# LayerNorm of a 2048x2048x2048 matmul: the opening rows' last chunk of A is transposed by the DMA and used last, and row tile 5 is loaded and transposed ahead of gamma and beta

## The chip, the cores and the metric

The kernel runs on one core of one Trainium2 chip. Five engines work side by side, each in its own order: TensorE (PE, with its weight loads as PEld), VectorE (DVE), ScalarE (ACT), GpSimd (POOL) and SyncE (SP), which here issues most of the transfers; 16 DMA engines move the data. The metric is the time of one execution in device microseconds (us), as a median over runs.

## The reference

```python
m, k, n = 2048, 2048, 2048          # a: (m, k), b: (k, n), float32
x = np.matmul(a, b)
mean = np.mean(x, axis=-1, keepdims=True)
var = np.var(x, axis=-1, keepdims=True)
normalized = (x - mean) / np.sqrt(var + eps)
return (gamma * normalized + beta).astype(np.float32)
```

## The kernel before, in words

The 2048 rows of the output are 16 row tiles of 128. N is cut into 4 quarters of 512 columns, K into 16 steps `kt` of 128, and four steps make a chunk. One matmul (`mm`, L85) adds one `kt` of one row tile and one quarter, 128x512, into a bank of PSUM, of which there are eight. A and B arrive in float32 and are multiplied in float16. B stays in SBUF as `b16`. A must stand with K on the partitions, so its tiles are transposed into `at`, two row tiles to a buffer.

While B is still arriving, the first five row tiles (R = 5, the opening rows) are worked on together, so that each piece of B that lands feeds five matmuls. Their A comes in chunks of 512 columns: `load_a1` and `load_a2` load to the staging buffers (`stg`, six of 512 KB) and VectorE casts to `a16s` (L186, L194). Then `turn` transposes on TensorE against an identity (L243) and ScalarE copies the result from PSUM to `at` (L245). B comes through `load_b2`, two `kt` of one quarter at a time, 512 KB, cast by VectorE (L205). SP issues the loads strictly in the order of the code; each waits until the staging buffer that it is to fill has been cast.

The order in the opening: chunk 0 of quarters 0, 1 and 2 for the five rows, each put aside into `x` in SBUF by ScalarE (`put_aside`, L261). Then the whole of quarter 3 (`MAIN`), with the transposes of chunks 1, 2 and 3 placed between its matmuls by `spots`; it is copied out by `evacuate` (ScalarE L95, and VectorE's statistics L96). Then chunks 1 to 3 of quarters 0 and 1, step by step over the five rows first and row by row at the end (`k_row`), with the remaining pieces of B asked for at hand-set places by `bring`. A finished quarter is added to the part put aside and its statistics taken (`add_rest`, VectorE L265 and L266). Quarter 2 is done row by row in the last loop of the opening, which also closes each row: `stats` (L102, L104 on VectorE, a square root L106 on ScalarE) and `queue_norm`, which queues the row's normalization in halves on a backlog.

The other eleven row tiles follow one by one, four quarters of 16 matmuls each. After each quarter `evacuate` runs and `drain(1)` issues one half of a queued row: two passes of VectorE (`centre` L111, `scale` L117) and a store. Their A is loaded by GpSimd's queue with a cast to float16 on the way (L345, three buffers `a16`), and transposed by one DMA for a whole row, 128x2048 (`turn_ahead`, L428, issued by SP two tiles ahead). A copy of one column on GpSimd (`gate`, L255) lets these loads start only when the last piece of B has landed. gamma and beta are broadcast to 128 partitions by two loads on SP (L335, L336) behind the last load of B. The last row tile has an ending of its own (`finish_row`).

The order of every engine is the order of the code (a manual schedule). What the change touches: `load_b2` L201 to L206, the loading loop L222 to L230, `bring` L248 to L255, the loops of `MAIN` and of the quarters L308 to L333, the loading of rows L342 to L345, `turn_ahead` L424 to L431 and the closing loop L432 to L436.

Of the kernel before, what the change touches and what calls it, by code (L numbers as in the profile page):

```python
# [10 lines left out]
FP16 = mybir.dt.float16  # L11
AluOp = mybir.AluOpType
# [4 lines left out]
def kernel(  # L17
# [21 lines left out]
    n_kc = n_kt // KC  # L39
    R = 5  # L40
    ASIDE, MAIN = (0, 1, 2), 3
# [10 lines left out]
    a16p = ctx.enter_context(tc.tile_pool(name="a16p", bufs=3))  # L52
# [22 lines left out]

    def new_pair(g):
        pair[g] = atp.tile([P, 2, n_kt, P], FP16, tag="at", name=f"at{g}")

    def at(i):
        return pair[i // 2][:, i % 2]  # L80

    def mm(i, q, kt, first, last):
        if (i, q) not in acc:
            acc[i, q] = bank(f"acc{i}_{q}")
        nc.tensor.matmul(  # L85
            acc[i, q], at(i)[:, kt, :], b16[:, kt, ds(q * NB, NB)],
            start=first, stop=last,
        )

    def evacuate(i, q):  # L90
        if xs[i] is None:
            xs[i] = xpool.tile([P, N], FP32, tag="x", name=f"x{i}")
            bnst[i] = stat.tile([P, n_nb, 6], FP32, tag="bnst", name=f"bnst{i}")
        qs = ds(q * NB, NB)
        nc.scalar.copy(xs[i][:, qs], acc[i, q])  # L95
        nc.vector.bn_stats(bnst[i][:, q, :], xs[i][:, qs])  # L96
# [3 lines left out]
    def stats(i):  # L100
        mv = stat.tile([P, 2], FP32, tag="mv", name=f"mv{i}")
        nc.vector.bn_aggr(mv, bnst[i])  # L102
        ve = stat.tile([P, 1], FP32, tag="ve", name=f"ve{i}")
        nc.vector.tensor_tensor(ve, mv[:, 1:2], eps_t, AluOp.add)  # L104
        sq = stat.tile([P, 1], FP32, tag="sq", name=f"sq{i}")
        nc.scalar.activation(sq, ve, ActFn.Sqrt)  # L106
        return mv, sq

    def centre(i, q, mv):
        qs = ds(q * NB, NB)  # L110
        nc.vector.scalar_tensor_tensor(  # L111
            xs[i][:, qs], xs[i][:, qs], mv[:, 0:1], gamma_b[:, qs],
            AluOp.subtract, AluOp.mult)

    def scale(i, q, rstd):
        qs = ds(q * NB, NB)
        nc.vector.scalar_tensor_tensor(  # L117
            xs[i][:, qs], xs[i][:, qs], rstd, beta_b[:, qs],
            AluOp.mult, AluOp.add)

    def store(i, q0, nq):
        s = ds(q0 * NB, nq * NB)
        nc.sync.dma_start(out[ts(i, P), s], xs[i][:, s])

    def inv(i, sq):
        rstd = stat.tile([P, 1], FP32, tag="rstd", name=f"rstd{i}")
        nc.vector.reciprocal(rstd, sq)
        return rstd

    def queue_norm(i, mv, sq):  # L130

        got = {}

        def piece(q0):
            def run():
                centre(i, q0, mv)
                centre(i, q0 + 1, mv)
                if q0 == 0:
                    got["rstd"] = inv(i, sq)
                scale(i, q0, got["rstd"])  # L140
                scale(i, q0 + 1, got["rstd"])
                store(i, q0, 2)
            return run

        backlog.extend(piece(q) for q in range(0, n_nb, 2))
# [20 lines left out]
    a16_of = {}  # L166
# [15 lines left out]
    def load_a1(i, c):  # L182
        st = half_stage()
        nc.sync.dma_start(st, a[ts(i, P), ts(c, KW)])  # L184
        a16_room(i, c)
        nc.vector.tensor_copy(a16_of[i, c], st)  # L186

    def load_a2(i, c):
        st = stg.tile([P, 2, NB], FP32, tag="st", name=f"sta{i}_{c}")
        nc.sync.dma_start(  # L190
            st, a[ds(i * P, 2 * P), ts(c, KW)].rearrange("(t p) k -> p t k", p=P))
        for m in (0, 1):
            a16_room(i + m, c)
        nc.vector.tensor_copy(held["a"][:, ds(i % KC, 2), :], st)  # L194
# [3 lines left out]
        nc.sync.dma_start(st, b[ts(k, P), 0:NB])  # L198
        nc.vector.tensor_copy(b16[:, k, 0:NB], st)  # L199

    def load_b2(k, q):  # L201
        st = stg.tile([P, 2, NB], FP32, tag="st", name=f"stb{q}_{k}")
        nc.sync.dma_start(
            st, b[ds(k * P, 2 * P), ds(q * NB, NB)].rearrange("(t p) n -> p t n", p=P))
        nc.vector.tensor_copy(b16[:, k:k + 2, ds(q * NB, NB)], st)  # L205
        return st  # L206

    pairs = [list(range(i, min(i + 2, R))) for i in range(0, R, 2)]

    def load_pair(j, c):  # L210
        if len(pairs[j]) == 2:
            load_a2(pairs[j][0], c)
        else:
            load_a1(pairs[j][0], c)
# [3 lines left out]
    for q in ASIDE[1:]:  # L218
        load_b2(0, q)
        load_b2(2, q)  # L220
    load_pair(0, 1)
    for c in range(n_kc):  # L222
        load_b2(c * KC, MAIN)
        if c + 1 < n_kc:
            load_pair(0 if c > 0 else 1, c + 1)
        load_b2(c * KC + 2, MAIN)
        if c + 1 < n_kc:
            if c > 0:
                load_pair(1, c + 1)
            load_pair(2, c + 1)  # L230

    warm = bank("warm")

# [4 lines left out]
    def turn(rows, c):  # L238
        n = len(rows)
        t_ps = psum.tile([P, n, KC, P], FP16, tag="ps", name=f"tps{rows[0]}_{c}")  # L240
        for m, i in enumerate(rows):
            for j in range(KC):
                nc.tensor.transpose(t_ps[:, m, j, :], a16_of[i, c][:, ts(j, P)], ident)  # L243
        i0 = rows[0]
        nc.scalar.copy(  # L245
            pair[i0 // 2][:, ds(i0 % 2, n), ds(c * KC, KC), :], t_ps)

    later = [(k, q) for q in ASIDE for k in range(0 if q == MAIN else KC, n_kt, 2)]  # L248

    def bring(n):  # L250
        for _ in range(n):
            k, q = later.pop(0)
            st = load_b2(k, q)
            if not later:
                nc.gpsimd.tensor_copy(gate, st[:, 0, 0:1])  # L255

    def put_aside(p, q):
        if xs[p] is None:
            xs[p] = xpool.tile([P, N], FP32, tag="x", name=f"x{p}")
            bnst[p] = stat.tile([P, n_nb, 6], FP32, tag="bnst", name=f"bnst{p}")  # L260
        nc.scalar.copy(xs[p][:, ds(q * NB, NB)], acc.pop((p, q)))  # L261

    def add_rest(p, q):
        qs = ds(q * NB, NB)
        nc.vector.tensor_tensor(xs[p][:, qs], acc[p, q], xs[p][:, qs], AluOp.add)  # L265
        nc.vector.bn_stats(bnst[p][:, q, :], xs[p][:, qs])  # L266
# [23 lines left out]
    for q in ASIDE[1:]:  # L290
# [3 lines left out]
        for p in range(R):  # L294
            for kt in range(2, KC):
                mm(p, q, kt, False, kt == KC - 1)
            put_aside(p, q)


    spots = {(0, 4): 0, (1, 1): 1, (1, 4): 2}  # L300
    for h in (0, 1):
# [3 lines left out]
            if (h, p) in spots:  # L305
                turn(pairs[spots[h, p]], 1)
    spots = {(1, 4): 0, (2, 4): 1, (3, 1): 2}
    for kt in range(KC, n_kt - KC):  # L308
        for p in range(R):
            mm(p, MAIN, kt, False, False)  # L310
            if (kt % KC, p) in spots:
                turn(pairs[spots[kt % KC, p]], kt // KC + 1)
    for kt in range(n_kt - KC, n_kt - 2):
        for p in range(R):
            mm(p, MAIN, kt, False, False)
    for p, n in enumerate((1, 1, 0, 1, 0)):
        for kt in (n_kt - 2, n_kt - 1):
            mm(p, MAIN, kt, False, kt == n_kt - 1)
        bring(n)
        evacuate(p, MAIN)  # L320


    for q, k_row, ahead, asked in (
            (0, n_kt - KC, 7, (0, 0, 1, 0, 1)), (1, 2 * KC, 2, (0, 1, 1, 1, 1))):
        bring(ahead)
        for kt in range(KC, k_row):
            for p in range(R):
                mm(p, q, kt, kt == KC, False)
        for p in range(R):
            for kt in range(k_row, n_kt):  # L330
                mm(p, q, kt, False, kt == n_kt - 1)
            bring(asked[p])
            add_rest(p, q)  # L333
    assert not later
    nc.sync.dma_start(gamma_b, gamma.unsqueeze(0).to_broadcast([P, N]))  # L335
    nc.sync.dma_start(beta_b, beta.unsqueeze(0).to_broadcast([P, N]))  # L336
    if eps_ap is not None:
# [1 line left out]
    else:  # L339
        nc.vector.memset(eps_t, eps_val)  # L340

    a16 = {}  # L342
    for i in range(R, n_mt):
        a16[i] = a16p.tile([P, K], FP16, tag="a16", name=f"a16_{i}")
        nc.gpsimd.dma_start(a16[i], a[ts(i, P), :])  # L345


    rows_gb = [stg.tile([2, 2, NB], FP32, tag="st", name=f"gb{h}") for h in (0, 1)]
# [72 lines left out]
        queue_norm(i, mv, sq)  # L421
        drain(1)

    def turn_ahead(t):  # L424
        if R <= t < n_mt:
            if t % 2 == 0:
                new_pair(t // 2)
            nc.sync.dma_start_transpose(at(t), a16[t])  # L428

    turn_ahead(R)  # L430
    turn_ahead(R + 1)  # L431
    for p in range(R):  # L432
        for kt in range(KC, n_kt):
            mm(p, ASIDE[2], kt, kt == KC, kt == n_kt - 1)
        add_rest(p, ASIDE[2])
        queue_norm(p, *stats(p))  # L436
    for i in range(R, n_mt):
        last = i == n_mt - 1
        turn_ahead(i + 2)
# [49 lines left out]
```

## Time and profile before

| | us |
|---|---|
| median of 3 runs (lowest to highest) | 245.42 (245.38 to 245.78) |
| the profiled execution | 245.69 |
| its span in the trace | 243.7 |
| TensorE matmuls, busy | 235.0 (96%) |
| VectorE busy | 173.0 (71%) |
| ScalarE busy | 55.1 (23%) |
| GpSimd busy | 12.6 (5%) |

In the profile a line such as L85 is the line of the kernel that issued the instruction, `out<-in` are the tiles it writes and reads. A group's row gives count, busy time and the mean duration of one in ns, then the time its engine had been idle before it and who ended that. Durations of pipelined matmuls overlap, so the mean of one (379 ns) is longer than the step from one to the next.

### The profile page before, as it was taken

What the parts mean: (1) busy time and instruction counts of PE and PEld (TensorE: products, weight loads), DVE (VectorE), ACT (ScalarE), POOL (GpSimd) and SP (SyncE); (2) the same over time, 40 slices, a digit from 0 to 9 for tenths busy, and PEclk for the clock granted to TensorE, in tenths of its full rate; (3) what the DMA queues carried; (4) which work ended last, traced back from release to release, by engine and by line L of the source; (5) the groups of instructions that cost most, each with busy time, mean ns of one, the idle gap of its engine ahead of it and who ended that gap; (6) DMA issues with size and microseconds to landing.
All of it is one profiled execution on the core that took longest, in us unless ns stands there. A gap on an engine that the chain in (4) does not pass through costs nothing.

```text
span 243.7 us, 2983 instructions
## 1 busy us (share of the span) xinstructions
PE 235.0 (96%) x1137; PEld 108.3 (44%) x1137; DVE 173.0 (71%) x304; ACT 55.1 (23%) x104; POOL 12.6 (5%) x19
## 2 busy tenths in 40 slices
PE   6899999999999999999999999999999999999991
PEld 2344555444444444444444444444444444444440
DVE  1544454969997679999999995937558392946771
ACT  2466445500000011112121211112111121112132
POOL 0000000000210100000000000036000000000000
PEclk9999999999999999999999999999999999999996
DMA  4999999999999998888999797683907145120405
GB/s 122 393 389 384 384 350 392 386 335 370 360 266 204 150 139 242 237 186 251 241 224 256 143 290 177 192 202 74 256 5 180 78 115 146 58 114 0 175 1 172
DMA packets 41190, 52.64 MB, mean 216 GB/s; under 512 B 24404, under 2 KB 24404, under 8 KB 40920
## 3 DMA queue, kind: packets, MB, share of 16 engines
q1 hardware_dynamic: 39592, 46.68, 59.1%
q0 software_dynamic: 1584, 5.77, 15.3%
q8 instruction: 9, 0.15, 0.3%
q14 instruction: 5, 0.04, 0.1%
HBM read 35.67 MB, written 16.78 MB: 215 GB/s over the span
## 4 chain that ended last, share of the span: by engine, by line
PE 93%; DMA 2%; ACT 1%; DVE 1%; SPq 0%; issue 0%
PE acc L85 91%; DMA st<-in_a_dram 2%; PE tps L243 2%; ACT x L408 1%; DVE bnst L373 0%; PE y L396 0%; DVE a16s L186 0%; PE warm L236 0%; SPq L198 0%; SPq L184 0%; PE ms_ps L391 0%; ACT mv_last L389 0%; DVE mv_last L388 0%; ACT lead L392 0%
## 5 line engine op out<-in xcount | busy, mean ns | idle before, releaser
L85 PE MATMUL acc<-b,at 128*128 128x512 f16 x1024 | 223.2, 379 | 1.0 <-DVE b L199 0.9
L85 PEld LDWEIGHTS <-at 128*128 128x128 f16 x1024 | 99.6, 98 | 119.3 <-ACT at L245 1.3
L96 DVE BATCH_NORM_STATS2 bnst<-x 128x6 f32<-128x512 f32 x48 | 32.9, 689 | 33.9 <-ACT x L95 33.8
L95 ACT COPY x<-acc 128x512 f32<-128x512 f32 x48 | 27.7, 588 | 108.8 <-PE acc L85 107.5
L117 DVE SCALAR_TENSOR_TENSOR x<-x,rstd,beta_b 128x512 f32<-128x512 f32 x62 | 43.8, 747 | 0.6
L111 DVE SCALAR_TENSOR_TENSOR x<-x,mv,gamma_b 128x512 f32<-128x512 f32 x60 | 42.0, 741 | 0.0
L205 DVE CAST b<-stb 128x1024 f16<-128x1024 f32 x30 | 20.4, 688 | 11.0 <-DMA stb<-in_b_dram 10.9
L106 ACT ACTIVATE sq<-ve 128x1 f32<-128x1 f32 x15 | 3.0, 203 | 51.1 <-DVE ve L104 51.1
L245 ACT COPY at<-tps 128x512 f16<-128x512 f16 (+1 forms) x14 | 10.6, 769 | 14.3 <-PE tps L243 14.0
L265 DVE TENSOR_TENSOR x<-acc,x 128x512 f32<-128x512 f32 x15 | 10.3, 685 | 3.3 <-PE acc L85 3.3
L345 POOL DMA_DIRECT2D a<-in_a_dram x11 | 6.4, 583 | 91.1 <-DMA at<-a 90.8
L266 DVE BATCH_NORM_STATS2 bnst<-x 128x6 f32<-128x512 f32 x15 | 10.4, 695 | 0.5
L261 ACT COPY x<-acc 128x512 f32<-128x512 f32 x15 | 7.6, 607 | 5.1 <-PE acc L85 5.1
L186 DVE CAST a16s<-st 128x512 f16<-128x512 f32 x8 | 3.4, 427 | 6.4 <-DMA st<-in_a_dram 6.2
L243 PE MATMUL tps<-ident,a16s 128*128 128x128 f16 x80 | 6.8, 220 | 0.9 <-DVE a16s L186 0.8
L236 PE MATMUL warm<-zeros 128*128 128x512 f16 x19 | 6.2, 462 | 1.2 <-DVE zeros L152 1.2
L243 PEld LDWEIGHTS <-a16s 128*128 128x128 f16 x80 | 5.2, 98 | 4.7 <-DVE a16s L186 2.6
L194 DVE CAST a16s<-sta 128x1024 f16<-128x1024 f32 x6 | 4.2, 694 | 4.1 <-DMA sta<-in_a_dram 3.4
L357 POOL TENSOR_SCALAR gb<-gb 1x1024 f32<-1x1024 f32 x2 | 5.5, 2764 | 0.0
L102 DVE BATCH_NORM_AGGREGATE mv<-bnst 128x2 f32<-128x24 f32 x15 | 4.0, 264 | 0.5
L236 PEld LDWEIGHTS <-zeros 128*128 128x128 f16 x19 | 2.0, 115 | 4.2 <-issue 2.6
L255 POOL COPY gate<-stb 128x1 f32<-128x1 f32 x1 | 0.2, 183 | 63.5 <-DMA stb<-in_b_dram 63.5
(31 smaller groups left out, 22.8 us busy)
## 6 DMA issues: line engine op xcount, KB each, us to landing
stb<-in_b_dram SPq DMA_DIRECT2D x30, 512.0 KB, 6.5
out_dram<-x SPq DMA_DIRECT2D x30, 512.0 KB, 3.0
a<-in_a_dram POOLq DMA_DIRECT2D x11, 512.0 KB, 6.7
sta<-in_a_dram SPq DMA_DIRECT2D x6, 512.0 KB, 6.3
st<-in_a_dram SPq DMA_DIRECT2D x8, 256.0 KB, 7.4
st<-in_b_dram SPq DMA_DIRECT2D x4, 256.0 KB, 6.6
gamma_b<-in_gamma_dram SPq DMA_DIRECT2D x1, 1024.0 KB, 7.2
beta_b<-in_beta_dram SPq DMA_DIRECT2D x1, 1024.0 KB, 9.2
```

The costliest lines, as they stand in the source:

```text
L85: nc.tensor.matmul(acc[i, q], at(i)[:, kt, :], b16[:, kt, ds(q * NB, NB)], start=first, stop=last,)
L95: nc.scalar.copy(xs[i][:, qs], acc[i, q])
L96: nc.vector.bn_stats(bnst[i][:, q, :], xs[i][:, qs])
L111: nc.vector.scalar_tensor_tensor(xs[i][:, qs], xs[i][:, qs], mv[:, 0:1], gamma_b[:, qs], AluOp.subtract, AluOp.mult)
L117: nc.vector.scalar_tensor_tensor(xs[i][:, qs], xs[i][:, qs], rstd, beta_b[:, qs], AluOp.mult, AluOp.add)
L205: nc.vector.tensor_copy(b16[:, k:k + 2, ds(q * NB, NB)], st)
L236: nc.tensor.matmul(warm if to is None else to, zeros[:, 0:P], zeros, start=True, stop=True)
L243: nc.tensor.transpose(t_ps[:, m, j, :], a16_of[i, c][:, ts(j, P)], ident)
L245: nc.scalar.copy(pair[i0 // 2][:, ds(i0 % 2, n), ds(c * KC, KC), :], t_ps)
L261: nc.scalar.copy(xs[p][:, ds(q * NB, NB)], acc.pop((p, q)))
L265: nc.vector.tensor_tensor(xs[p][:, qs], acc[p, q], xs[p][:, qs], AluOp.add)
L266: nc.vector.bn_stats(bnst[p][:, q, :], xs[p][:, qs])
```

## The change

The A of the opening rows' chunk 3 is still loaded and cast as before, but no longer transposed by TensorE: five DMA transposes of 128x512 (`turn_last`) write it to `at`, issued by SP between loads of B. Chunk 3's loads stand later among the loads, behind the first pieces of quarter 0. Since chunk 3 comes later, the main quarter now stops after chunk 2 and is put aside, and so is quarter 0 a second time (`add_part`, which adds to what is already aside, without statistics). Quarters 1 and 2 are done to their end. Chunk 3 of quarters 3 and 0 is multiplied last, row by row, and closes the rows.

The remaining 14 loads of B are issued one after another, with no hand-set places, and ScalarE casts them instead of VectorE. Row tile 5 is loaded once B's quarter 2 has landed, with four loads of B still behind it, and transposed ahead of gamma and beta; the loads of row tiles 6 and on wait for the very last load of B.

```diff
-    def load_b2(k, q):
+    def load_b2(k, q, cast=nc.vector.tensor_copy):
...
-        nc.vector.tensor_copy(b16[:, k:k + 2, ds(q * NB, NB)], st)
+        cast(b16[:, k:k + 2, ds(q * NB, NB)], st)
...
-    for c in range(n_kc):
+    K3 = n_kt - KC
+    for c in range(n_kc - 1):
         load_b2(c * KC, MAIN)
-        if c + 1 < n_kc:
+        if c + 2 < n_kc:
             load_pair(0 if c > 0 else 1, c + 1)
         load_b2(c * KC + 2, MAIN)
-        if c + 1 < n_kc:
+        if c + 2 < n_kc:
             if c > 0:
                 load_pair(1, c + 1)
             load_pair(2, c + 1)
+    load_b2(KC, 0)
+    load_b2(KC + 2, 0)
+    for j in range(len(pairs)):
+        load_pair(j, n_kc - 1)
+        if j < 2:
+            load_b2(2 * KC + 2 * j, 0)
+    load_b2(KC, 1)
+    load_b2(KC + 2, 1)
...
+    def turn_last(i):
+        nc.sync.dma_start_transpose(at(i)[:, ds(K3, KC), :], a16_of[i, n_kc - 1])
...
+    def add_part(p, q):
+        qs = ds(q * NB, NB)
+        nc.vector.tensor_tensor(xs[p][:, qs], acc.pop((p, q)), xs[p][:, qs], AluOp.add)
...
+    def part(q, k0, k1, k_row, done):
+        for kt in range(k0, k_row):
+            for p in range(R):
+                mm(p, q, kt, kt == k0, False)
+        for p in range(R):
+            for kt in range(k_row, k1):
+                mm(p, q, kt, kt == k0, kt == k1 - 1)
+            done(p, q)
...
-    for p, n in enumerate((1, 1, 0, 1, 0)):
-        for kt in (n_kt - 2, n_kt - 1):
-            mm(p, MAIN, kt, False, kt == n_kt - 1)
-        bring(n)
-        evacuate(p, MAIN)
+    for p in range(R):
+        for kt in (K3 - 2, K3 - 1):
+            mm(p, MAIN, kt, False, kt == K3 - 1)
+        put_aside(p, MAIN)
...
+    later = [(k, 1) for k in range(2 * KC, n_kt, 2)]
+    later += [(k, 2) for k in range(KC, n_kt, 2)]
+    later += [(k, q) for q in (MAIN, 0) for k in range(K3, n_kt, 2)]
+    for n, (k, q) in enumerate(later):
+        for i in range(2 * n, min(2 * n + 2, R)):
+            turn_last(i)
+        st = load_b2(k, q, nc.scalar.copy)
+        if (k, q) in ((n_kt - 2, 2), later[-1]):
+            nc.gpsimd.tensor_copy(gate, st[:, 0, 0:1])
+        if (k, q) == (n_kt - 2, 2):
+            load_row(R)
+    turn_ahead(R)
+    part(0, KC, K3, K3 - 2, add_part)
+    part(1, KC, n_kt, K3, add_rest)
+    part(2, KC, n_kt, K3, add_rest)
     nc.sync.dma_start(gamma_b, gamma.unsqueeze(0).to_broadcast([P, N]))
     nc.sync.dma_start(beta_b, beta.unsqueeze(0).to_broadcast([P, N]))
...
-    for i in range(R, n_mt):
-        a16[i] = a16p.tile([P, K], FP16, tag="a16", name=f"a16_{i}")
-        nc.gpsimd.dma_start(a16[i], a[ts(i, P), :])
+    for i in range(R + 1, n_mt):
+        load_row(i)
...
-    turn_ahead(R)
     turn_ahead(R + 1)
-    for p in range(R):
-        for kt in range(KC, n_kt):
-            mm(p, ASIDE[2], kt, kt == KC, kt == n_kt - 1)
-        add_rest(p, ASIDE[2])
+    def close_opening(p, q):
+        add_rest(p, q)
         queue_norm(p, *stats(p))
+    part(MAIN, K3, n_kt, K3, add_rest)
+    part(0, K3, n_kt, K3, close_opening)
```

More of the change, by code (lines that the diff above doesn't have):

```diff
@@ L246, in turn @@
             pair[i0 // 2][:, ds(i0 % 2, n), ds(c * KC, KC), :], t_ps)
[L248 to L255, printed above, removed]
+    def turn_last(i):
+        nc.sync.dma_start_transpose(at(i)[:, ds(K3, KC), :], a16_of[i, n_kc - 1])
     def put_aside(p, q):
@@ L307, with load_row, turn_ahead @@
     spots = {(1, 4): 0, (2, 4): 1, (3, 1): 2}
-    for kt in range(KC, n_kt - KC):
+    for kt in range(KC, K3 - 2):
         for p in range(R):
             mm(p, MAIN, kt, False, False)
-            if (kt % KC, p) in spots:
+            if kt < 2 * KC and (kt % KC, p) in spots:
                 turn(pairs[spots[kt % KC, p]], kt // KC + 1)
-    for kt in range(n_kt - KC, n_kt - 2):
-        for p in range(R):
-            mm(p, MAIN, kt, False, False)
-    for p, n in enumerate((1, 1, 0, 1, 0)):
-        for kt in (n_kt - 2, n_kt - 1):
-            mm(p, MAIN, kt, False, kt == n_kt - 1)
-        bring(n)
-        evacuate(p, MAIN)
[L323 to L334, printed above, removed]
+    for p in range(R):
+        for kt in (K3 - 2, K3 - 1):
+            mm(p, MAIN, kt, False, kt == K3 - 1)
+        put_aside(p, MAIN)
+    a16 = {}
+    def load_row(i):
+        a16[i] = a16p.tile([P, K], FP16, tag="a16", name=f"a16_{i}")
+        nc.gpsimd.dma_start(a16[i], a[ts(i, P), :])
+    def turn_ahead(t):
+        if R <= t < n_mt:
+            if t % 2 == 0:
+                new_pair(t // 2)
+            nc.sync.dma_start_transpose(at(t), a16[t])
+    later = [(k, 1) for k in range(2 * KC, n_kt, 2)]
[13 more added lines that the diff above has]
+    part(2, KC, n_kt, K3, add_rest)
     nc.sync.dma_start(gamma_b, gamma.unsqueeze(0).to_broadcast([P, N]))
@@ L340 @@
         nc.vector.memset(eps_t, eps_val)
-    a16 = {}
-    for i in range(R, n_mt):
-        a16[i] = a16p.tile([P, K], FP16, tag="a16", name=f"a16_{i}")
-        nc.gpsimd.dma_start(a16[i], a[ts(i, P), :])
+    for i in range(R + 1, n_mt):
+        load_row(i)
     rows_gb = [stg.tile([2, 2, NB], FP32, tag="st", name=f"gb{h}") for h in (0, 1)]
@@ L422, in close @@
         drain(1)
[L424 to L428, printed above, removed]
-    turn_ahead(R)
     turn_ahead(R + 1)
-    for p in range(R):
-        for kt in range(KC, n_kt):
-            mm(p, ASIDE[2], kt, kt == KC, kt == n_kt - 1)
-        add_rest(p, ASIDE[2])
+    def close_opening(p, q):
+        add_rest(p, q)
         queue_norm(p, *stats(p))
+    part(MAIN, K3, n_kt, K3, add_rest)
+    part(0, K3, n_kt, K3, close_opening)
     for i in range(R, n_mt):
```

## The prediction, made before the changed kernel ran

> **What bounds the kernel now.** I read the chain that ended last first, then its pieces in order of time, then the waits of TensorE.
>
> ```profile
> PE 93%; DMA 2%; ACT 1%; DVE 1%; SPq 0%; issue 0%
> ...
> 10.54 14.68 PE acc L85 x67
> ...
> 36.09 0.45 PE tps L243 x8
> 36.53 1.08 PE acc L85 x5
> 37.61 0.45 PE tps L243 x8
> 38.06 0.43 PE acc L85 x2
> 38.49 0.22 PE tps L243 x4
> 38.72 195.77 PE acc L85 x907
> ```
>
> The first line is the page's summary of the chain, the others are the start, duration and work of single pieces. From 10.54 us TensorE is the chain: 907 matmuls stand in one piece of 195.77 us, 0.2158 us each, with nothing between them. The last chunk's transposes stand in the chain too: 8, 8 and 4 of them take 0.45, 0.45 and 0.22 us.
>
> ```profile
> PE warm L236 <- DVE zeros L152: 1.2, 1, 1.2
> PE acc L85 <- DVE b L199: 0.9, 1, 0.9
> PE tps L243 <- DVE a16s L186: 0.8, 1, 0.8
> PE y L396 <- ACT lead L392: 0.4, 1, 0.4
> ```
>
> These are all waits of TensorE: three in the opening's first microseconds, one in the tail. So between 10.54 and 234 us time falls only if TensorE does less, and it rises only if the change makes TensorE wait.
>
> ```profile
> 40.00:50.00 10.00, 10.00 (x49) 4.52 (x47) 7.48 (x13) 3.83 (x6) 0.00 (x0) 1.00 1.04 382
> 50.00:60.00 10.00, 10.00 (x48) 4.58 (x47) 8.55 (x14) 0.00 (x0) 0.00 (x0) 1.00 1.00 353
> 60.00:70.00 10.00, 10.00 (x48) 4.50 (x47) 9.51 (x16) 0.00 (x0) 2.36 (x4) 1.00 0.99 346
> ```
>
> Columns: the stretch, its length, busy time of PE, PEld, DVE, ACT and POOL, granted clock, DMA share, GB/s. While TensorE is full, the DMA engines are full as well (share 1.04, 382 GB/s). The opening thus runs with two full resources side by side, and the change moves work from the first to the second.
>
> **What is removed.** 20 transposes of chunk 3: 0.45 + 0.45 + 0.22 = 1.12 us of the chain. The number of matmuls stays 1024. If nothing takes the freed place, the time falls by 1.12 us.
>
> **How early the operands come.** The loads are served one after the other; VectorE's casts show when they land.
>
> ```profile
> 32.01 0.69 DVE L205 CAST b<-stb 128x1024 f16<-128x1024 f32 x1 [0.82 <-DMA stb<-in_b_dram]
> 50.08 0.69 DVE L205 CAST b<-stb 128x1024 f16<-128x1024 f32 x1 [0.63 <-DMA stb<-in_b_dram]
> ...
> L245 ACT COPY at<-tps 128x1024 f16<-128x1024 f16 x6 | 6.1, 1012 | 7.5 <-PE tps L243 7.5
> L95 ACT COPY x<-acc 128x512 f32<-128x512 f32 x48 | 27.7, 588 | 108.8 <-PE acc L85 107.5 <-DMA out_dram<-x 1.3
> ```
>
> The first cast takes B's rows 8 and 9 of the main quarter, the second comes 13 loads of 512 KB and one of 256 KB later: 18.07 / 13.5 = 1.34 us a load. The order up to the first of them is unchanged, and in the new order the load for quarter 1, kt 14 and 15, is also 13.5 loads behind it. It lands at 50.08 plus whatever the five DMA transposes ahead of it cost. Its cast is now ScalarE's, which the trace does not show in this shape: below by VectorE's 0.69, above by two 512-wide copies, 1.18; I take 1.01 from the copy of the same size. Ready: 51.09 + 5T, with T the time that one transpose of 128x512 holds up the loads.
>
> TensorE needs it when it has done, after 36.09, 10 matmuls of the main quarter, 40 of quarter 0 and 42 of quarter 1: 36.09 + 92 x 0.2158 = 55.94. So up to 4.85 us can be absorbed, T = 0.97. By the same count kt 12 is needed at 55.51 and ready at 49.75 + 5T, kt 10 at 53.35 against 48.41 + 4T, kt 8 at 51.20 against 47.07 + 2T. Kt 14 is the tightest. Quarter 2's first pair is ready at 52.43 + 5T and needed at 59.83, later ones have more. Ahead of the transposes the slack is over 1 us everywhere: the load for kt 10 of the main quarter, for instance, moves one place forward and is cast by 34.04, against 36.09.
>
> **What a transpose costs.** The trace has only full-row ones (128x2048, four times as much).
>
> ```profile
> L428 SPq DMA_TRANSPOSE at<-a x11: 1869/3254/5823, 72.5 to 198.2; - x11
> DMA to landing us min/median/max: 4.4/5.0/13.6
> ...
> 79.91 0.53 POOL L345 DMA_DIRECT2D a<-in_a_dram x1 [12.08 <-DMA at<-a]
> 82.37 0.53 POOL L345 DMA_DIRECT2D a<-in_a_dram x1 [1.93 <-DMA at<-a]
> 93.50 0.53 POOL L345 DMA_DIRECT2D a<-in_a_dram x1 [10.60 <-DMA at<-a]
> 106.83 0.53 POOL L345 DMA_DIRECT2D a<-in_a_dram x1 [12.80 <-DMA at<-a]
> ...
> 101.37 3.21 SPq L428 DMA_TRANSPOSE at<-a  x1
> ...
> 104.00:105.00 1.00, 1.00 (x6) 0.44 (x5) 1.00 (x3) 0.00 (x0) 0.00 (x0) 1.00 1.17 218
> ```
>
> GpSimd's loads wait for transposes to free a buffer, so their starts date the landings. The first two transposes end 2.46 us apart though each takes 4.4 us or more from issue to landing: latency overlaps, and what a following transfer feels is 2.46 us, or 0.62 a quarter. The window inside the transpose issued at 101.37 agrees: 218 GB/s at full share, so 0.131 MB take 0.60 us. Lower end: as fast as a load of that size, 1.34 / 4 = 0.34. Upper end: the third one's distance, 93.50 - 82.37 = 11.13, or 2.78. Three of these readings lie near 0.6, so I take T = 0.62. 5T = 3.1 us against 4.85: hidden behind the lead of the loads, with 1.75 us to spare. The Trainium skill (Advanced Engine Details and Errata, X-Bar Transpose) says that such a transpose is as fast as a regular DMA; this trace does not agree (218 against 382 GB/s). By the rule 5T would be an estimated 1.7 us, and the rival below that holds up the loads would lose its chance.
>
> SP issues one full row in 3.25 us (median), so a quarter in 0.81 and five in 4.1. Each waits for its cast. Two go out behind the quarter 1, kt 6 load, two behind kt 8, one behind kt 10. The loads queued behind them on SP are delayed by less than 4.85 even if all of it counts, and some six loads' work is already in the queues. The load for kt 14 also waits until the first transpose has landed.
>
> **The other moves.** Five statistics of the main quarter move to the end, and five more adds come there. With 40 matmuls still to do (8.63 us), VectorE has more than that:
>
> ```profile
> L266 DVE BATCH_NORM_STATS2 bnst<-x 128x6 f32<-128x512 f32 x15 | 10.4, 695 | 0.5
> L265 DVE TENSOR_TENSOR x<-acc,x 128x512 f32<-128x512 f32 x15 | 10.3, 685 | 3.3 <-PE acc L85 3.3
> L102 DVE BATCH_NORM_AGGREGATE mv<-bnst 128x2 f32<-128x24 f32 x15 | 4.0, 264 | 0.5
> ...
> 150.00:155.00 5.00, 5.00 (x25) 2.27 (x24) 2.65 (x7) 0.79 (x2) 0.00 (x0) 1.00 0.90 198
> ```
>
> Ten rows at 1.38 us and five closings make some 16 us, so VectorE is about 6 us further behind when row tile 5 starts. Row tile 5's first bank was that of the main quarter's third row. Quarter 2's first row ends at 69.3; five pairs and then two and a half of the main quarter later it is free: 79.7. TensorE asks for it at 81.4. Later banks have more room, being asked for again eight quarters (27.6 us) after they were filled. The lag is worked off in the gaps VectorE has from 150 us on. Cost 0; if the 1.7 us cover were gone, TensorE would stand there. ScalarE's 14 casts (14 us) fall into a stretch where it is idle (0.00 from 50 to 70), again cost 0.
>
> Row tile 5's load moves ahead of four of B's, its transpose ahead of gamma and beta:
>
> ```profile
> 65.10 0.18 POOL L255 COPY gate<-stb 128x1 f32<-128x1 f32 x1 [63.52 <-DMA stb<-in_b_dram]
> 65.65 2.18 POOL L345 DMA_DIRECT2D a<-in_a_dram  x3 [0.37 <-DVE x L265]
> 72.46 12.78 SPq L428 DMA_TRANSPOSE at<-a  x3
> ```
>
> The gate opens at 50.08 + 6 x 1.34 + 3.1 = 61.2; with 0.55 to the issue and 6.81 (65.65 to 72.46) the row is there at 68.6. As long as the first one (72.46 to 79.91) the transpose ends at 76.0, against 81.4. SP waits for that load with gamma, beta and the next transposes queued behind; gamma and beta go out some 13 us later than before and are wanted by VectorE only after its 16 us of adds, about 92. Cost 0.
>
> **Sum.** 245.69 us of the profiled execution (243.7 span, 1.99 around it) less 1.12 is 244.57. The median of the runs shown is 0.27 below the profiled one: 245.42 - 1.12 = 244.3.
>
> **The rivals.**
>
> *The transposes hold up the loads* (the other side). If each holds the queue as long as the one at 101.37 held its buffer, (106.83 - 101.37) / 4 = 1.37, five make 6.83, TensorE waits 1.98 us at quarter 1, kt 14, and the time is 246.3. It is slower than before from T above 1.19 (0.97 plus 1.12 / 5), and at 2.78 it gives 9.05 us of waiting, 253.4. For it: the 11.13 us of the third one, next to other transfers. Against: the 2.46 us and the 218 GB/s. Chance 0.24, of which 0.04 within 0.2% of before.
>
> *Each transpose costs its full latency.* The trace's shortest landing is that of the last row's stores:
>
> ```profile
> out_dram<-x SPq DMA_DIRECT2D x4, 256.0 KB, 2.5
> ```
>
> With T = 2.5 us TensorE waits 12.5 - 4.85 = 7.65: 252.0. Against it: landings 2.46 us apart for four times the data. Chance 0.04. The Trainium skill (DMA: Bandwidth & Descriptors, Anatomy of one DMA) gives a fixed 2.0 us for a DMA from GpSimd's path, an estimated 2.3 for this size; it also calls it a latency, and so does the trace.
>
> *Row tile 5 is late.* If its transpose takes the 13.6 us of the slowest, it lands at 82.2, TensorE waits 0.8 and the time is 245.1, no change. Chance 0.05.
>
> *VectorE gives the bank late.* At 1.85 us a row in place of 1.38 the bank is free at 82.9: 1.5 us of waiting, 245.8, again within 0.2%. Nothing in the profile makes a pair that slow. Chance 0.02.
>
> *The change gives nothing:* the freed 1.12 us turn into a wait of the same size for B elsewhere in the opening, 245.4. Slack of over 1 us at each load speaks against it. Chance 0.03.
>
> **How the numbers follow.** Forecast 0.62, rivals together 0.38. Faster by over 0.2% (about 0.5 us, what a measurement here can tell from no change): 0.62; within: 0.04 + 0.05 + 0.02 + 0.03 = 0.14; slower: 0.20 + 0.04 = 0.24. The likeliest case alone spans 244.0 to 244.7; the range has to take in the loads held up at 1.37, so 244.0 to 246.4.
>
> **What would show it.** Right: no wait of the accumulating matmuls on casts, on the opening's transposes or on adds; 60 transposes left on TensorE; casts for quarter 1, kt 14, ending near 54 us. Wrong: a wait of TensorE for a ScalarE cast between 50 and 56 us (T too small), for row tile 5 near 81, or for an add there.

## The result, and the profile after

The changed kernel takes 244.38 us (median of 8 runs, 244.04 to 245.1), the kernel before on the same chip 245.49 (8 runs, 245.2 to 245.86): a ratio of 0.9958, 95% interval 0.9947 to 0.9969, or 1.1 us less. The profiled execution took 244.29 us with a span of 242.2, where the one before had 245.69 and 243.7. Ratios here are taken over fast runs alone, which leaves out one execution (249.53 us, of `e6_gb_first`).

The chain that ended last comes first again, in order of time (start, duration, work); the first line is the page's summary.

```profile
PE 94%; DMA 2%; ACT 1%; DVE 1%; issue 0%; DVEq 0%
...
9.97 14.67 PE acc L85 x67
...
32.48 0.22 PE tps L252 x4
32.70 13.61 PE acc L85 x63
...
46.50 0.69 DVE x L268
...
47.24 8.36 PE acc L85 x38
55.60 0.04 issue
55.64 177.59 PE acc L85 x822
```

TensorE is still the chain, and the pieces of 0.45, 0.45 and 0.22 us that the last chunk's transposes had in it are gone. In their place are two interruptions. At 46.3 us quarter 1 wants a bank which VectorE's `add_part` (L268) has not yet read. At 55.6 it wants quarter 1's `kt` 14, which ScalarE is just casting. How much they cost is seen beside a second execution of the same kernel, in which both are missing:

```profile
33.23 0.22 PE tps L252 x4
33.46 200.09 PE acc L85 x927
```

From the same point, the end of the last transposes on TensorE, 927 matmuls take 200.09 us here. In the first execution they would have ended at 32.70 + 200.09 = 232.79 and ended at 55.64 + 177.59 = 233.23: 0.44 us were lost. TensorE itself is idle for no more than 0.08 and 0.04 us of this; the rest is overlap between neighbouring matmuls that is missing at a stop.

So the two profiled executions, before and after, compare as follows. TensorE's matmuls ended at 38.72 + 195.77 = 234.49 before and at 233.23 after, 1.26 us earlier: 1.12 by the transposes, 0.57 because the dense part happened to begin at 9.97 in place of 10.54, less the 0.44. (The opening up to there is the same code, and over the traces of this study it begins between 9.97 and 10.94.) Of the difference of 1.40 between the two times the remaining 0.14 lies behind the matmuls: a tail 0.24 shorter, and 0.10 more outside the span.

The groups of instructions by line (count | busy us, mean ns | idle before) show that the work on TensorE is what was announced:

```profile
L85 PE MATMUL acc<-b,at 128*128 128x512 f16 x1024 | 223.0, 379 | 0.1
...
L252 PE MATMUL tps<-ident,a16s 128*128 128x128 f16 x60 | 5.4, 225 | 0.1
...
L205 ACT CAST b<-stb 128x1024 f16<-128x1024 f32 x14 | 14.6, 1045 | 16.8 <-DMA stb<-in_b_dram 16.8
```

1024 matmuls, 60 transposes left, and ScalarE's 14 casts at 1.045 us each. Of SyncE's queue the stretch with the five transposes, then the transposes' durations in ns (min/median/max):

```profile
37.67 2.70 SPq L258 DMA_TRANSPOSE at<-a16s  x2
40.47 0.53 SPq L203 DMA_DIRECT2D stb<-in_b_dram  x1
41.09 4.46 SPq L258 DMA_TRANSPOSE at<-a16s  x2
45.60 0.58 SPq L203 DMA_DIRECT2D stb<-in_b_dram  x1
46.27 1.20 SPq L258 DMA_TRANSPOSE at<-a16s  x1
...
L258 SPq DMA_TRANSPOSE at<-a16s x5: 1201/1347/2601, 37.7 to 46.3; - x5
```

SP stands 1.2 to 2.6 us at each transpose, 0.53 to 0.58 at a load. The five take 2.70 + 4.46 + 1.20 = 8.36 us of it. What this does to the loads is dated by the casts, first VectorE's, then ScalarE's (start, duration, idle before and its releaser):

```profile
31.02 0.69 DVE L205 CAST b<-stb 128x1024 f16<-128x1024 f32 x1 [0.82 <-DMA stb<-in_b_dram]
...
45.29 0.69 DVE L205 CAST b<-stb 128x1024 f16<-128x1024 f32 x1 [2.14 <-DMA stb<-in_b_dram]
...
54.54 1.04 ACT L205 CAST b<-stb 128x1024 f16<-128x1024 f32 x1 [0.75 <-DMA stb<-in_b_dram]
```

The first is the main quarter's `kt` 8, the second quarter 1's `kt` 6, on which VectorE waits 2.14 us with the adds L268 queued behind it: the first interruption. The third is quarter 1's `kt` 14. It ends at 55.58. The last 822 matmuls take 177.59 of the 200.09 us, so undisturbed TensorE would have begun them 22.50 us behind 32.70, at 55.20: the second.

Row tile 5 is dated by GpSimd, whose fourth load waits for its transpose, and by SP's issue of that transpose:

```profile
63.39 0.19 POOL L357 COPY gate<-stb 128x1 f32<-128x1 f32 x1 [61.81 <-DMA stb<-in_b_dram]
63.95 0.72 POOL L340 DMA_DIRECT2D a<-in_a_dram  x1 [0.37 <-issue]
...
80.35 0.53 POOL L340 DMA_DIRECT2D a<-in_a_dram  x1 [9.67 <-DMA at<-a]
...
70.95 6.88 SPq L346 DMA_TRANSPOSE at<-a  x1
```

The row is there at 70.95 and transposed by 80.3. Row tile 5 begins 118 matmuls (822 less its and the later rows' 704) after 55.64, at 81.1. Only 0.8 us lie between.

### The profile page after: what moved, and what is told of

It reads as the page before. It is cut to its first block, busy times and chain, and to the rows that moved or that the text cites. A ratio compares the mean times of both kernels' runs of the same rounds, so it can differ in the third digit from the quotient of the medians.

```text
span 242.2 us, 2970 instructions
## 1 busy us (share of the span) xinstructions
PE 235.4 (97%) x1117; PEld 107.5 (44%) x1117; DVE 171.6 (71%) x300; ACT 66.0 (27%) x115; POOL 12.5 (5%) x20
## 4 chain that ended last, share of the span: by engine, by line
PE 94%; DMA 2%; ACT 1%; DVE 1%; issue 0%; DVEq 0%
PE acc L85 91%; DMA st<-in_a_dram 2%; PE tps L252 2%; PE warm L245 1%; ACT x L437 1%; DVE bnst L402 0%; DVE x L268 0%; PE y L425 0%; DVE a16s L186 0%; PE ms_ps L420 0%; ACT mv_last L418 0%; DVE mv_last L417 0%; ACT lead L421 0%; DVEq L268 0%
## 5 line engine op out<-in xcount | busy, mean ns | idle before, releaser
L85 PE MATMUL acc<-b,at 128*128 128x512 f16 x1024 | 223.0, 379 | 0.1
L85 PEld LDWEIGHTS <-at 128*128 128x128 f16 x1024 | 99.8, 98 | 120.2 <-ACT at L254 1.1
L117 DVE SCALAR_TENSOR_TENSOR x<-x,rstd,beta_b 128x512 f32<-128x512 f32 x62 | 44.4, 756 | 0.6
L111 DVE SCALAR_TENSOR_TENSOR x<-x,mv,gamma_b 128x512 f32<-128x512 f32 x60 | 42.9, 756 | 0.0
L95 ACT COPY x<-acc 128x512 f32<-128x512 f32 x43 | 24.5, 585 | 66.9 <-PE acc L85 66.9
L272 DVE TENSOR_TENSOR x<-acc,x 128x512 f32<-128x512 f32 x20 | 13.6, 678 | 13.6 <-PE acc L85 13.6
L205 DVE CAST b<-stb 128x1024 f16<-128x1024 f32 x16 | 11.1, 694 | 12.5 <-DMA stb<-in_b_dram 12.5
L205 ACT CAST b<-stb 128x1024 f16<-128x1024 f32 x14 | 14.6, 1045 | 16.8 <-DMA stb<-in_b_dram 16.8
L264 ACT COPY x<-acc 128x512 f32<-128x512 f32 x20 | 10.2, 605 | 7.5 <-PE acc L85 7.5
L254 ACT COPY at<-tps 128x512 f16<-128x512 f16 (+1 forms) x11 | 8.1, 742 | 10.8 <-PE tps L252 10.5
L245 PE MATMUL warm<-zeros 128*128 128x512 f16 x19 | 7.4, 534 | 1.2 <-DVE zeros L152 1.2
L252 PEld LDWEIGHTS <-a16s 128*128 128x128 f16 x60 | 4.0, 100 | 3.6 <-DVE a16s L186 2.2
L252 PE MATMUL tps<-ident,a16s 128*128 128x128 f16 x60 | 5.4, 225 | 0.1
```

The source lines that it names most:

```text
L85: nc.tensor.matmul(acc[i, q], at(i)[:, kt, :], b16[:, kt, ds(q * NB, NB)], start=first, stop=last,)
L111: nc.vector.scalar_tensor_tensor(xs[i][:, qs], xs[i][:, qs], mv[:, 0:1], gamma_b[:, qs], AluOp.subtract, AluOp.mult)
L117: nc.vector.scalar_tensor_tensor(xs[i][:, qs], xs[i][:, qs], rstd, beta_b[:, qs], AluOp.mult, AluOp.add)
L205: cast(b16[:, k:k + 2, ds(q * NB, NB)], st)
L245: nc.tensor.matmul(warm if to is None else to, zeros[:, 0:P], zeros, start=True, stop=True)
L254: nc.scalar.copy(pair[i0 // 2][:, ds(i0 % 2, n), ds(c * KC, KC), :], t_ps)
```

## The experiments

Each edit is made against the changed kernel. All compare with the kernel before, run on the same chip beside them.

| kernel | median us (lowest to highest, runs) | ratio to before, 95% interval |
|---|---|---|
| `e1_pe_turn` | 245.68 (245.05 to 247.05, 12) | 1.0004 [0.9986, 1.0022] |
| `e2_no_turn` | 244.21 (244.09 to 244.61, 5) | 0.9940 [0.9927, 0.9953] |
| `e3_twice` | 250.87 (250.13 to 251.38, 4) | 1.0204 [1.0184, 1.0225] |
| `e4_late_turn` | 244.63 (244.22 to 245.16, 6) | 0.9954 [0.9940, 0.9968] |
| `e5_row5_back` | 246.37 (245.89 to 247.26, 10) | 1.0029 [1.0014, 1.0044] |
| `e6_gb_first` | 246.88 (245.18 to 249.53, 10) | 1.0041 [1.0014, 1.0068] |
| `e7_one_turn` | 244.67 (1 run) | none |
| `e8_one_place` | 244.88 (243.84 to 247.28, 10) | 0.9991 [0.9957, 1.0025] |
| `e9_five_places` | 244.67 (243.90 to 246.57, 10) | 0.9968 [0.9947, 0.9990] |
| `after_again` | 244.57 (244.07 to 246.53, 12) | 0.9964 [0.9947, 0.9981] |
| `e9_again` | 244.58 (244.28 to 246.04, 7) | 0.9958 [0.9943, 0.9973] |
| `e10_five_later` | 244.57 (244.20 to 245.91, 11) | 0.9961 [0.9949, 0.9972] |

**Where the gain comes from.** `e1_pe_turn` gives the 20 transposes back to TensorE and leaves everything else changed.

```diff
-        for i in range(2 * n, min(2 * n + 2, R)):
-            turn_last(i)
...
-    part(0, KC, K3, K3 - 2, add_part)
+    part(0, KC, K3, K3 - 2, add_part, {(7, 4): 0, (8, 4): 1, (9, 4): 2})
```

(`part` calls `turn` for chunk 3 at these places, with VectorE copying to `at`.)

> The changed kernel with only the five DMA transposes undone: chunk 3 of the opening rows is transposed by TensorE again (20 transposes between the matmuls of quarter 0, copied out of PSUM by VectorE). Theory (the gain is the 1.12 us of TensorE's transposes, less about 0.3 us of waits that the DMA transposes cause at 46 and 55 us): the chain has 20 transposes more, the loads come about 5 us earlier, no waits; some 0.8 us slower than the changed kernel, 245.2, ratio to before 0.998 to 1.000. Rival (the gain comes from the new order of quarters, casts and row tile 5): the time stays at 244.4, ratio 0.996.

Measured: ratio 1.0004, the whole gain gone, just above the 0.998 to 1.000 expected. The chain of that kernel:

```profile
42.07 0.45 PE tps L252 x8
...
43.59 0.45 PE tps L252 x8
...
45.12 0.22 PE tps L252 x4
45.34 188.65 PE acc L85 x874
```

The three pieces of 0.45, 0.45 and 0.22 us stand in it again, with matmuls on both sides and no wait. From the start of the dense part to the last matmul it takes 45.34 + 188.65 - 10.06 = 223.93 us, the kernel before 234.49 - 10.54 = 223.95, the changed kernel's undisturbed execution 33.46 + 200.09 - 10.73 = 222.82: 1.11 less. Between the ratios of this and of the changed kernel lie 0.0046, or 1.13 us of 245.5. The gain is the transposes' time on TensorE; the rest of the change, the new order of quarters, the casts on ScalarE and the place of row tile 5 taken together, neither brings nor costs anything that can be measured.

**What the DMA transposes cost.** `e2_no_turn` issues none at all.

```diff
-            acc[i, q], at(i)[:, kt, :], b16[:, kt, ds(q * NB, NB)],
+            acc[i, q], at(i)[:, kt - KC if i < R and kt >= n_kt - KC else kt, :], b16[:, kt, ds(q * NB, NB)],
...
-        for i in range(2 * n, min(2 * n + 2, R)):
-            turn_last(i)
```

> The changed kernel without any transpose of chunk 3: the opening rows multiply chunk 2 of A a second time in its place, all loads and casts stay. Theory (one transpose holds up the loads by about 1.1 us, not 0.62): the cast for quarter 1, kt 14, starts near 49 us after an equal start, 5.4 us before the changed kernel's 54.54; the two waits of TensorE near 46 and 55 us go; time 0.2 to 0.4 us below the changed kernel, 244.1. Rival (0.62 each, the loads were late for another reason): that cast moves by only 3 us. Rival (the transposes cost TensorE much more than the chain shows): time below 243.5.

(`at(i)` is read at chunk 2 in place of chunk 3: the kernel leaves chunk 3 of the opening rows out.)

Measured: ratio 0.9940; 0.0018 (0.4 us) below the changed kernel's, with intervals that just overlap. Its chain runs unbroken, `33.14 200.09 PE acc L85 x927`. The changed kernel's first trace lost about as much, 0.44 us, and its second nothing, so by these traces there is no more than that to win by making the transposes cheaper. In windows over the stretch of the transposes (stretch, length, busy PE, PEld, DVE, ACT, POOL, granted clock, DMA share, GB/s), first this kernel, then the changed one:

```profile
42.00:43.00 1.00, 1.00 (x6) 0.48 (x5) 0.41 (x1) 0.00 (x0) 0.00 (x0) 1.00 1.04 406
43.00:45.00 2.00, 2.00 (x11) 0.89 (x10) 0.71 (x2) 0.00 (x0) 0.00 (x0) 1.00 1.05 395
45.00:48.00 3.00, 3.00 (x16) 1.37 (x14) 2.82 (x5) 1.20 (x2) 0.00 (x0) 1.00 1.05 390
```

```profile
42.00:43.00 1.00, 1.00 (x6) 0.49 (x5) 0.54 (x1) 0.00 (x0) 0.00 (x0) 1.00 2.29 206
43.00:45.00 2.00, 2.00 (x11) 0.88 (x9) 0.16 (x1) 0.00 (x0) 0.00 (x0) 1.00 1.27 40
45.00:48.00 3.00, 2.92 (x15) 1.27 (x13) 2.71 (x5) 0.23 (x1) 0.00 (x0) 1.00 1.06 285
```

With the transposes the queues stay occupied (share over 1) and move 40 GB/s for two microseconds, where they move 395 without. The packet records of this trace show what occupies them: between 43.5 and 45 us no packet of a load (2 KB) is under way. The five transposes are 2560 packets of 256 bytes, 18 ns each in the median, but 38 of these took 0.8 to 1.5 us, and they ended together, at 43.6 or at 45.3 us. The second trace has one such group, 20 packets that ended at 44.4. So in this trace the loads stand behind the transposes' own packets; what holds those up, and what lets them go, is not shown.

`e3_twice` doubles the suspected cost: each transpose is followed by a second one, into a spare buffer.

```diff
+    extra = atp.tile([P, 2, n_kt, P], FP16, tag="at", name="extra")
...
             turn_last(i)
+            nc.sync.dma_start_transpose(
+                extra[:, i % 2, ds(i // 2 * KC, KC), :], a16_of[i, n_kc - 1])
```

> The changed kernel with each of the five DMA transposes followed by a second one of the same source into a buffer that nobody reads: ten instead of five. Theory (1.1 us each, the lead of the loads is already used up): all of the added 5.4 us turns into waits of TensorE before quarter 1, kt 14: 249.8, from 248.5 to 251 (SP's waits for landings can add some). Rival (0.62 each): 3.1 us later with 1.7 in hand, 245.8. Rival (latency overlaps wholly): no change, 244.4.

Measured: 250.87, where 249.8 was expected, in a range of 248.5 to 251. Its waits (in all, times, longest) and the part of its chain ahead of the long piece:

```profile
PE acc L85 <- ACT b L205: 3.9, 2, 3.2
```

```profile
46.61 0.43 SPq L258
...
47.09 1.26 SPq L356
...
54.26 0.58 SPq L203
...
54.89 5.86 DMA stb<-in_b_dram
...
60.78 1.05 ACT b L205
...
61.87 177.59 PE acc L85 x822
```

The chain no longer leads through TensorE: it goes over SP's issues of the transposes and of their doubles (L258, L356) to a load of B, its cast, and only then to the matmuls. They end at 61.87 + 177.59 = 239.46, against 33.34 + 200.09 = 233.43 without a wait: 6.03 us. Five transposes are all but hidden, ten are not.

`e4_late_turn` issues the same five later, behind quarter 1's `kt` 10 and behind quarter 1's `kt` 14.

```diff
-        for i in range(2 * n, min(2 * n + 2, R)):
+        for i in {2: (0, 1), 4: (2, 3, 4)}.get(n, ()):
             turn_last(i)
```

> The changed kernel with the five DMA transposes moved back in SP's order: rows 0 and 1 behind quarter 1's kt 10 load, rows 2, 3 and 4 behind its kt 14 load. Theory (the waits come from where they stand, each costs 1.1 us): the cast for quarter 1, kt 14, about 3.3 us earlier, quarter 1's kt 6 about 1.5 us earlier; no waits near 46 and 55 us; 0.2 to 0.3 us faster than the changed kernel, 244.1. Rival: the last transposes land behind their matmuls (57 to 59 us) and TensorE waits there instead, 244.4 to 245.5.

Measured: ratio 0.9954. Its chain is unbroken (`33.35 200.09 PE acc L85 x927`), so the small stalls can be placed away, but the time cannot be told from the changed kernel's.

**Row tile 5.** `e5_row5_back` loads and transposes it where the kernel before did, behind the last of B and behind gamma and beta. `e6_gb_first` moves only its transpose back behind gamma and beta.

```diff
-        if (k, q) in ((n_kt - 2, 2), later[-1]):
+        if (k, q) == later[-1]:
             nc.gpsimd.tensor_copy(gate, st[:, 0, 0:1])
-        if (k, q) == (n_kt - 2, 2):
-            load_row(R)
-    turn_ahead(R)
...
-    for i in range(R + 1, n_mt):
+    for i in range(R, n_mt):
         load_row(i)
...
+    turn_ahead(R)
     turn_ahead(R + 1)
```

> The changed kernel with row tile 5 put back in its old place: its load waits for the last load of B, its transpose stands behind gamma and beta. Theory (the early place is needed, since in the changed kernel the transpose frees its buffer at 80.35 us and TensorE wants the row at about 81.2): the load goes out near 69.5, lands near 76.5, the transpose ends near 84 or later, TensorE waits 3 us or more; 247 to 249. Rival (the place is free, as other transfers only wait their turn): under 0.3 us of waiting, 244.4 to 244.7.

```diff
-    turn_ahead(R)
...
+    turn_ahead(R)
     turn_ahead(R + 1)
```

> The changed kernel with only the order of gamma, beta and row tile 5's transpose as before: the row is still loaded early, its transpose is issued behind gamma, beta and their small rows. Theory (gamma and beta, 1 MB each, then share the DMA engines with the row's load, and the row's transpose is issued behind them): the row lands 2 to 4 us later, the transpose ends at 82 to 84, TensorE waits 1 to 3 us; 245.4 to 247.4. Rival (gamma and beta fit in front because SP waits for the row's load anyway): the transpose ends at 80 to 81 as before, 244.4.

Both are slower than before. The wait of `e5_row5_back`, 1.9 us, was smaller than expected, and so was its time; `e6_gb_first` came out in its range. Its runs scatter widely (245.18 to 249.53), and its one trace (245.72 us) shows a wait of 0.9 us, which does not explain all of the median. First the wait and the chain of `e5_row5_back`, then those of `e6_gb_first`:

```profile
PE acc L85 <- DMA at<-a: 1.9, 1, 1.9
...
68.86 7.32 DMA a<-in_a_dram
...
76.20 7.02 DMA at<-a
```

```profile
PE acc L85 <- DMA at<-a: 0.9, 1, 0.9
...
63.29 10.24 DMA a<-in_a_dram
...
73.55 8.92 DMA at<-a
```

TensorE stands until 83.27 and 82.52. Without the early place the gain is lost and more: 0.0071 between the ratios of `e5_row5_back` and the changed kernel is 1.7 us, about its wait of 1.9. In `e6_gb_first` the row is loaded as early as in the changed kernel (its gate copy at 62.74), yet the row lands only at 73.5. Gamma and beta are now issued at 61 us, beside it; that they delay it is an argument, no run separates it.

**Is it a price for each transpose, or one standstill?** If each costs 0.9 us, one costs 0.9; if the first ones stop the transfers, one costs as much as two or more.

```diff
-        for i in range(2 * n, min(2 * n + 2, R)):
-            turn_last(i)
+        if n == 0:
+            turn_last(0)
```

(and rows 1 to 4 take chunk 2 again, as in `e2_no_turn`.)

> The changed kernel with the DMA transpose of row 0 alone; rows 1 to 4 multiply chunk 2 of A a second time in place of chunk 3. Measure: from the cast of the main quarter's kt 8 load to the cast of quarter 1's kt 14 load it is 23.52 us in the changed kernel with five and 19.03 without any. Theory P (each transpose costs the loads the same, 0.9): 19.9. Theory S (the first transposes stop the transfers once, as the 43 to 45 us of the changed kernel's trace with 76 and 5 GB/s suggest, and each further one costs 0.4 or so): 21.5 or more, and the DMA rate falls under 100 GB/s for a microsecond or more.

```diff
-        for i in range(2 * n, min(2 * n + 2, R)):
+        for i in (range(R) if n == 2 else ()):
             turn_last(i)
```

> The changed kernel with all five DMA transposes at one place, behind quarter 1's kt 10 load. Theory P: the same 4.5 us for the loads behind them, quarter 1's kt 14 at 23.5 us after the main quarter's kt 8, but kt 8 and 10 undelayed; 244.2 to 244.5. Theory S with a stop for each group of transposes: one stop in place of three, kt 14 at 22 us or less; 244.1 to 244.4. In both the time stays within 0.2% of the changed kernel, and the wait near 46 us goes.

```diff
-        for i in range(2 * n, min(2 * n + 2, R)):
-            turn_last(i)
+        if n < R:
+            turn_last(n)
```

> The changed kernel with the five DMA transposes at five places: one ahead of each of quarter 1's kt 8, 10, 12 and 14 loads and of quarter 2's first. Theory P: four of them stand ahead of quarter 1's kt 14, 19.03 + 4 x 0.9 = 22.6 us; 244.2 to 244.5. Theory S with a stop at each place: 25 us or more and TensorE waits 1.5 us or more at quarter 1's kt 14, 245.5 or more. Theory S with one stop in all: 22 us.

> The changed kernel once more, beside the two next ones on the same chip: ratio to before 0.995 to 0.997 as measured first.

`e9_again` is `e9_five_places` unchanged, `e10_five_later` the same one place later each.

> The kernel with the transposes at five places once more. If its unbroken chain (no wait of TensorE behind 10.24 us) counts, 0.2 to 0.3 us below the changed kernel, ratio 0.994 to 0.996; if such waits are within the scatter, no difference.

```diff
-        for i in range(2 * n, min(2 * n + 2, R)):
-            turn_last(i)
+        if 0 < n <= R:
+            turn_last(n - 1)
```

> Five places again, each one load later: ahead of quarter 1's kt 10, 12 and 14 loads and of quarter 2's first two. If a transpose that stands alone costs the loads 0.45 us, quarter 1's kt 14 load is cast 20.0 to 20.4 us after the main quarter's kt 8 (three ahead of it), kt 6 of quarter 1 is not delayed, no waits; time as the kernel with five places, 0.994 to 0.996. If each costs 0.9: 21.7 us, still no waits, the same time.

The measure is the distance from VectorE's cast of the main quarter's `kt` 8 to ScalarE's of quarter 1's `kt` 14, both read from the timelines; 19.03 us without a transpose (`e2_no_turn`; 18.58 in `e1_pe_turn`).

| kernel | transposes ahead | distance us | each, over 19.03 |
|---|---|---|---|
| changed kernel, first trace | 5 | 23.52 | 0.90 |
| changed kernel, second trace | 5 | 22.11 | 0.62 |
| `e5_row5_back` | 5 | 22.98 | 0.79 |
| `e6_gb_first` | 5 | 22.40 | 0.67 |
| `e8_one_place` | 5 | 23.43 | 0.88 |
| `e9_five_places` | 4 | 20.57 | 0.39 |
| `e9_again` | 4 | 22.46 | 0.86 |
| `e10_five_later` | 3 | 20.42 | 0.46 |
| `e4_late_turn` | 2 | 19.79 | 0.38 |
| `e7_one_turn` | 1 | 19.31 | 0.28 |
| `e3_twice` | 10 | 29.65 | 1.06 |

The last column is rough. Against the 18.58 of `e1_pe_turn` every distance would be 0.45 longer. And it counts only the transposes that SP issues ahead of the load for kt 14, while those behind a load can delay it too: quarter 1's kt 6 is issued ahead of the first transpose, yet its cast began 2.83 us behind that of kt 4 in the changed kernel's first trace, 1.36 in `e2_no_turn`.

`e7_one_turn` fits neither theory: one transpose cost 0.28 (0.73 against the 18.58), below 0.9 and far from 2.5. It did come with a standstill, again one microsecond long:

```profile
43.00:44.00 1.00, 1.00 (x6) 0.48 (x5) 0.58 (x1) 0.00 (x0) 0.00 (x0) 1.00 2.34 237
44.00:45.00 1.00, 1.00 (x7) 0.46 (x5) 0.11 (x1) 0.00 (x0) 0.00 (x0) 1.00 0.37 36
```

`e8_one_place` came out where a price for each had put it (23.5 expected). `e9_five_places` missed all three of its expectations (22, 22.6, 25 or more) with 20.57; its second execution, 22.46, lies between the first two. `e10_five_later` fell at the edge of where 0.45 for a single one had put it. What remains open is when the transfers stop and for how long. The same kernel gave 22.11 and 23.52, and 20.57 and 22.46. The traces of `e9_five_places` and of `e9_again` between 43 and 46 us:

```profile
43.00:44.00 1.00, 1.00 (x6) 0.43 (x5) 0.15 (x1) 0.00 (x0) 0.00 (x0) 1.00 0.27 45
44.00:45.00 1.00, 1.00 (x6) 0.48 (x5) 0.76 (x2) 0.00 (x0) 0.00 (x0) 1.00 1.07 354
45.00:46.00 1.00, 1.00 (x7) 0.43 (x5) 1.00 (x2) 0.00 (x0) 0.00 (x0) 1.00 1.13 328
```

```profile
43.00:44.00 1.00, 1.00 (x6) 0.43 (x5) 0.28 (x1) 0.00 (x0) 0.00 (x0) 1.00 2.51 211
44.00:45.00 1.00, 1.00 (x6) 0.49 (x5) 0.41 (x1) 0.00 (x0) 0.00 (x0) 1.00 1.14 43
45.00:46.00 1.00, 1.00 (x7) 0.43 (x5) 0.00 (x0) 0.00 (x0) 0.00 (x0) 1.00 0.42 13
```

One lasts about a microsecond, the other two, and the second makes TensorE wait for adds (0.5 us in all). The DMA engines are not always occupied in it: their share is 0.27 in the first of these traces and 0.42 at the end of the other, as it is 0.37 with a single transpose. In both traces here SP stands at its third transpose meanwhile, from 41.56 for 2.13 us and from 42.89 for 3.96 us. None of these placements is measurably faster than the changed kernel: the ratios of `e4_late_turn`, both runs of the five places and `e10_five_later` lie between 0.9954 and 0.9968, the changed kernel's two at 0.9958 and 0.9964. All five in one place (`e8_one_place`) hold SP for 8.15 us and make TensorE wait 0.4 us for the cast; its runs scatter from 243.84 to 247.28, and its ratio doesn't tell it from the kernel before.

## Why the prediction was right

The forecast was 244.3 us; it is 244.38. That they agree to 0.1 us is in part luck: the interval of the ratio alone is 0.5 us wide, and the first execution lost 0.44 us that the forecast put at nothing. Two of the prediction's own signs of being wrong, a wait for a ScalarE cast between 50 and 56 us and one for an add, showed in that execution, too short to turn the result; the second execution had neither.

- **The sum.** Its one term, 1.12 us of transposes off TensorE, is what the kernel gains, shown by giving them back (`e1_pe_turn`) and by leaving the DMA's out as well (`e2_no_turn`). That nothing would take the freed place held to within 0.44 us in one execution and wholly in the other.
- **The lead of the loads.** 1.75 us were to spare for quarter 1's `kt` 14; in the first trace 0.38 us were missing, in the second (cast ended 54.60, wanted at 33.46 + 22.50 = 55.96) 1.36 were to spare. From the main quarter's `kt` 8 the cast was to end 51.09 + 3.1 - 32.01 = 22.18 us later, and ended 55.58 - 31.02 = 24.56 later. The 2.38 us are three terms: the 13.5 loads took 19.03 without any transpose, not 18.07 (0.96); T was 0.90, not 0.62 (five times 0.28, 1.39); the cast took 1.04, not 1.01 (0.03). On the other side TensorE wanted it 55.20 - 31.02 = 24.18 us later, not 23.93. So the threshold was not T = 0.97 but (4.85 - 0.96 - 0.03 + 0.25) / 5 = 0.82, and the first trace is over it. The traces with five transposes sort by it: at 0.88 and 0.90 TensorE stops for that cast, at 0.62 and 0.67 it doesn't; at 0.79 (`e5_row5_back`) the cast ended at 55.64, 0.07 late by the same count (33.07 + 22.50 = 55.57). Mechanism and place were right, the margin was not sure: it came out between -0.4 and 1.4 us, and it is luck on which side an execution falls.
- **T.** 0.62 lies within what five transposes showed (0.62 to 0.90) and at its low end. Of the readings given for it two lie near 0.6 (0.62 and 0.60), not three. Reading 2.46 us for a transpose of four times the size as 0.62 assumed that the price goes with the bytes. By SP it doesn't: 1.2 us or more for a quarter, not 0.81, and 8.36 for five in place of 4.1. By the rule of the Trainium skill (Advanced Engine Details and Errata, X-Bar Transpose), as fast as a regular DMA, it would be an estimated 0.34 each. Transposes that stood alone came near that in three traces of four (0.28 to 0.46), as did the two together ahead of kt 14 in `e4_late_turn` (0.38); five or ten in groups did not (0.62 to 1.06). No single number fits all.
- **The other side** (transposes hold up the loads) was the right rival to fear. Ten transposes lose 6.03 us in just that way; five lie at its edge.
- **Casts, adds, banks.** ScalarE's casts cost nothing. VectorE closed the opening's last row at 91.83, against "about 92", and no bank of row tile 5 came late. The add that held up a bank at 46.3 us was not foreseen: the prediction looked at the adds at the end and at quarter 1's loads for TensorE, but not at VectorE's in-order queue, in which `add_part` stands behind the cast of quarter 1's `kt` 6.
- **Row tile 5.** The gate opened at 63.39, not at 61.2, since the loads came later. The transpose took 9.4 us, not 7.45, beside the loads of row tiles 6 and 7, which GpSimd issues at 69.62. It ended at 80.3 against 76.0 forecast, with 0.8 us left instead of 5.4. The cost stayed 0, as predicted, but `e5_row5_back` and `e6_gb_first` show that a later place costs 0.9 to 1.9 us. The prediction had left open what the early place is worth; it is needed for the gain.

## What to carry to other kernels

Where one engine is the chain and has no gaps, work taken off it is worth its own time on that engine, and the question to work out is how much lead the stage has for what takes its place. Work the lead out as a distance between two instructions of one trace, and keep something for the spread between executions: the distance measured here differed by 1.4 and by 1.9 us between two executions of one kernel. The second resource, the DMA queues, was full too, and five small transposes used up 3.1 to 4.5 us of a lead of 4.1. Look at the issuing queue as well: five of them held SP for 8.36 us, twice what their bytes had suggested. Whether it is better to spread them out singly is not shown: three traces say so, a second execution of one of the kernels does not, and no placement changed the time measurably.

## What the runs showed of the hardware

- A DMA transpose of 128x512 in 2 bytes held SP for 1.2 to 2.6 us in the changed kernel's first trace (up to 3.96 in `e9_again`), a load of 512 KB issued between them 0.53 to 0.58. A full row of 128x2048 held it for 2.06 to 8.61 us (median 3.30) in the changed kernel.
- When the first transposes run among queued loads, the traffic falls from about 395 GB/s to 40 (43 to 45 us). In the changed kernel's first trace the DMA engines are occupied meanwhile, by packets of the transposes that take 0.8 to 1.5 us in place of 18 ns. It happens with a single transpose too (36 GB/s, there at a share of 0.37), and its length differs between executions of the same kernel. What starts and ends it was not settled.
- A row's transpose running beside GpSimd's loads took 9.4 us until its buffer was free (70.95 to 80.35).
